# A two-layer fp32 transformer kernel: first query block over halves of the inputs, spatial sums in banks of two groups, and the last rows' norm weights from a row made in layer A

## The chip, the core and the metric

The kernel runs on one core of one Trainium2 chip. The metric is the device time of one execution in microseconds (us). TensorE is called PE, VectorE DVE, ScalarE ACT, GpSimd POOL and SyncE SP.

## The reference

The input is x, 512 rows (tokens) of 1024 numbers, and a memory of 256 rows. Two layers follow each other; everything is fp32.

```python
def rmsnorm(x, g):
    xf = x.astype(jnp.float32)
    y = xf * lax.rsqrt(jnp.mean(xf * xf, axis=-1, keepdims=True) + RMS_EPS)
    return (y * g.astype(jnp.float32)).astype(x.dtype)

def chunked_spatial_gating(u, v, w_s, b_s, ln_g, ln_b):
    u = jax.nn.gelu(u)
    v = layernorm(jax.nn.gelu(v), ln_g, ln_b)
    vc = v.reshape(B, nc, CHUNK, A_GROUPS, A_GROUP_DIM)          # 4 chunks of 128, 6 groups of 128
    w = jnp.where(mask[None], w_s, jnp.zeros((), w_s.dtype))     # lower triangle
    s = jnp.einsum('gts,bcsgd->bctgd', w, vc) + b_s.T[None, None, :, :, None]
    return u * s.reshape(B, S, MAIN_WIDTH)

for layer in range(2):
    a = rmsnorm(h, ln_mix_pre[layer])
    mem_n = rmsnorm(mem, ln_mem[layer])
    if layer == 0:                       # "layer A"
        proj = a @ w_in_a[layer]         # 1024 -> u 768, v 768, q_mem 256
        main = chunked_spatial_gating(u, v, ...)
    else:                                # "layer B"
        main = forgetting_attention(q, k_s, v_s, log_f_s)
    mixed = jnp.concatenate([main, memory_attention(q_mem, mem_n, w_mem_kv[layer])], axis=-1)
    h = h + rmsnorm(mixed @ w_out[layer], ln_mix_post[layer])
    f = rmsnorm(h, ln_ffn_pre[layer])
    f = (silu(f @ w_ffn_gate[layer]) * (f @ w_ffn_up[layer])) @ w_ffn_down[layer]
    h = h + rmsnorm(f, ln_ffn_post[layer])
```

The last line of layer B is the kernel's end: each row of f is divided by its root mean square, multiplied column by column by 1024 weights ("norm weights", gains), and added to h.

## The kernel before

**Numbers in two parts.** Each fp32 operand is split in a high part (a copy rounded to fp32r, by ACT) and a low part (the rest, by DVE): `whi` and `wlo` of weights, `ahi` and `alo` of the normed inputs, `vhi` and `vlo` of the spatial values. `mm3` makes a product from three matmuls: high x high, low x high, high x low (L193 to L195, in the order that the profile's rows show).

**Layout.** h is kept turned: 8 tiles (index k) of 128 columns of the model by 512 rows. PSUM holds tiles of 128 x 512 in banks of three groups, `mm` and `lg` with three banks each and `tr` with two; a new tile of a group takes the bank whose turn it is and waits until its old content has been read. `idle(n, ...)` issues n matmuls on zeros whose result nobody reads (L88).

**Order.** Each engine has a queue of its own that it works through in order. A scheduler places the instructions in these queues, mostly as the program is written; `high_priority` moves some ahead, and `behind(...)` or `issue_after` places an instruction after a named one on its queue. Loads go through SP's queue.

**Start.** `layer_a` loads the weights of two query blocks (`raws`, each 128 x 1024, 512 KB; block 0 in two halves of 256 KB) and x (8 tiles of 256 KB) and multiplies them: `outs[0]` and `outs[1]` each get 8 products by `mm3`, input by input, both outputs for each input. The sum of squares of x (`acc`), its mean over columns (`st`, a matmul on `avg`), the root (`r`, POOL) and its spread over partitions (`rb`) follow, while PE goes on with the value blocks (`v`).

**Spatial sums.** For each of six groups `spatial(g)` makes two sums `s` of two chunks each (L735, L736). Ahead of them come a transpose of the layernorm's weights (`vcols`, L757), and the `rows` products with which `bsp`, the bias, is completed on DVE (L768). `gate_inputs(m)` makes the u of the next group on PE (`ps`), and DVE and ACT finish it (`u`).

**End.** The last product (w_down of layer B) has four blocks `tb` of 128 rows, each in two halves `dh` of 512 columns. `tail(tb)` makes the products `y` (PE), adds partial sums (DVE, L816), squares (ACT, L819, with the sum of squares in `ss`), completes the mean square `v` (DVE, L821), takes the root `r` (POOL, L262) and scales y by r (ACT, L840). In the last block the second half is done in two pieces of 256 columns, and y is scaled in pieces by DVE (L835) and ACT (L836). `give(tb - 1, ...)`, called after the next block's `tail`, transposes y into h's layout (`yt`, PE, L847), multiplies by the norm weights, which then are one number per partition, and adds to h (DVE, L852, 128 x 128 at a time), and stores (L1369, 256 KB a store; the last block 128 KB a store on SP and ACT in turn).

Of the kernel before, what the change touches and what calls it, by code (L numbers as in the profile page):

```python
# [15 lines left out]
P = 128  # L16
T = 512
D = 1024
# [22 lines left out]
def hybrid(ctx: ExitStack, tc: tile.TileContext, i: dict, out: bass.AP):  # L41
# [6 lines left out]
    sp = ctx.enter_context(tc.tile_pool(name="small", bufs=8))  # L48
    pp = ctx.enter_context(tc.tile_pool(name="psum", bufs=3, space=PSUM))
# [515 lines left out]

    def layer_a():
# [18 lines left out]
        tokens(0, 1)  # L585
        query_weights(1, 0, 1024)
        tokens(1, 2)
        tokens(2, 4)
# [3 lines left out]
        last_a = tuple(last_parts)  # L592
        vg, evacs = {}, []
# [28 lines left out]
        with tc.tile_pool(name="sgu", bufs=1) as lp:  # L622
# [105 lines left out]
            def spatial(g):  # L728
                t = temp("s", (P, TB, P))
                for tp2 in range(2):  # L730
                    o = ps("lg", (P, 2, 2, P), s="s")
                    hi, lo = vp[g // 2, tp2]
                    c = slice((g % 2) * P, (g % 2 + 1) * P)
                    for n in range(2):
                        PE.matmul(o[:, n, :, :], hi[:, n, c], ws[g], start=True, stop=True)  # L735
# [22 lines left out]
            V.tensor_copy(vcols, o)  # L758

# [25 lines left out]
    def tail_of(xs, load, ys, eps=None, last=False):  # L785
# [12 lines left out]
        def tail(tb, halfway=None):  # L798
# [4 lines left out]
            c = slice(tb, tb + 1)  # L803
            final = last and tb == TB - 1
            two = small("two", 1) if final else None
            at = [(0, 0, 4), (1, 0, 2), (1, 2, 4)] if final else [(0, 0, 4), (1, 0, 4)]
            for n, (dh, m0, m1) in enumerate(at):
                if m0 == 0:
                    o = ps("lg" if dh else "mm", s="y")
                cols = slice(m0 * P, m1 * P)  # L810
                for k in range(nk):
                    w = [part[:, m0:m1, :] for part in ws[k // 2, dh][k % 2]]
                    end = token_products(o[:, cols], xs[k], w, tb, k == 0, k == nk - 1)
                y = ys[tb][dh][:, cols]
                with urgent(tb):
                    V.tensor_add(y, o[:, cols], y)  # L816
# [3 lines left out]
                    if n == len(at) - 1:  # L820
                        V.scalar_tensor_tensor(out=v[:, c], in0=one, scalar=run, in1=eps[:, c] if eps is not None else rms_eps,  # L821
# [10 lines left out]
            if final:  # L832
                for m in (0, 2):
                    cols = slice(m * P, (m + 2) * P)
                    V.tensor_scalar_mul(ys[tb][1][:, cols], ys[tb][1][:, cols], r[:, c])  # L835
                    A.activation(ys[tb][0][:, cols], ys[tb][0][:, cols], AF.Copy, scale=r[:, c])  # L836
                return end
            with urgent(tb):
                for y in ys[tb]:
                    A.activation(y, y, AF.Copy, scale=r[:, c])  # L840

        return tail, ys

    def turned(ys, k, tbs, out):

        for n, tb in enumerate(tbs):
            PE.transpose(out[:, n * P : (n + 1) * P], ys[tb][k // 4][:, k % 4 * P : (k % 4 + 1) * P], ident)  # L847
# [510 lines left out]

    def give(tb, order, queues=(nc.sync,)):
# [79 lines left out]
```

## Time and profile before

| what | value |
|---|---|
| median of 3 runs | 1113.27 us (1113.27 to 1113.5) |
| the profiled execution | 1111.68 us, of which the span of its instructions 1110.0 us |
| PE, DVE, ACT, POOL busy | 99%, 81%, 60%, 2% of the span |
| moved by DMA | 118.13 MB, mean 106 GB/s |
| granted clock of TensorE | 0.999 |

The profiled execution is one of its own, 1.6 us below the median of the three timed ones; all places in the span below are of it. A row of the timeline has the start in us from the span's beginning, the busy time in us, the engine, the program's line, the operation, the tiles written and read, the shape, how many follow each other, and in brackets how long the engine was idle before and what ended that. A row of windows has, for each engine, the busy us and the instructions begun, then the clock of TensorE, the share in which the DMA engines were busy, and GB/s.

### The profile page before, as it was taken

The page shows a single profiled execution, that of the slowest core. Times are in us where ns is not written, and L with a number is a line of the kernel's source. Part 1 is how long each engine was busy: PE and PEld are TensorE (multiplying, and loading weights), DVE is VectorE, ACT ScalarE, POOL GpSimd, SP SyncE. Part 2 cuts the span into 40 slices and gives each one's busy share as a digit, 9 for nine tenths or more (in the row PEclk, how much of TensorE's full clock was granted, in tenths as well). Part 3 has the DMA queues.
Part 4 walks back from the last instruction along what each step waited for, and adds up shares of the span by engine and source line. Part 5 has one row for each costly group of instructions (what it writes and reads, how often), then busy time and mean ns, then how long its engine had stood idle before and what let it go on. Part 6 is the DMA issues. An engine that isn't in the chain of part 4 may idle for free.

```text
span 1110.0 us, 19527 instructions
## 1 busy us (share of the span) xinstructions
PE 1100.9 (99%) x7384; PEld 999.7 (90%) x7385; DVE 895.0 (81%) x1734; ACT 667.1 (60%) x1401; POOL 25.1 (2%) x41
## 2 busy tenths in 40 slices
PE   9999999999999999999999999999999999999998
PEld 6997889999899899998988897889999899899996
DVE  7879659897698598787868889868897698588775
ACT  7776578664366254477647667768665266254453
POOL 0000000000000000001000000000000000000000
PEclk9999999999999999999999999999999999999999
DMA  7521331334135133245222555431234134233222
GB/s 268 159 79 58 113 116 39 115 115 136 55 115 152 56 96 115 79 150 173 77 76 75 155 124 131 129 115 39 77 97 151 58 115 134 58 114 114 77 76 77
DMA packets 63558, 118.13 MB, mean 106 GB/s; under 512 B 5164, under 2 KB 39992, under 8 KB 63464
## 3 DMA queue, kind: packets, MB, share of 16 engines
q1 hardware_dynamic: 62584, 116.05, 34.4%
q8 instruction: 58, 0.95, 0.4%
q0 software_dynamic: 192, 0.52, 0.2%
q10 hardware_dynamic: 688, 0.31, 0.1%
q14 instruction: 36, 0.29, 0.1%
HBM read 104.71 MB, written 2.10 MB: 96 GB/s over the span
## 4 chain that ended last, share of the span: by engine, by line
PE 86%; DVE 3%; ACT 1%; issue 1%; DMA 0%; POOLq 0%; POOL 0%; DVEq 0%; ACTq 0%
PE y L193 10%; PE y L194 10%; PE y L195 10%; PE a L194 5%; PE a L195 5%; PE a L193 5%; PE ps L193 3%; PE ps L194 3%; PE ps L195 3%; PE x L194 3%; PE x L195 3%; PE x L193 3%; PE e L193 3%; PE e L194 3%; PE e L195 3%; PE tr L457 1%
## 5 line engine op out<-in xcount | busy, mean ns | idle before, releaser
L241 ACT CAST whi<-raw 128x512 fp32r<-128x512 f32 x460 | 277.2, 620 | 266.6 <-PE y L195 118.5
L241 DVE TENSOR_TENSOR wlo<-raw,whi 128x512 fp32r<-128x512 f32 x460 | 306.3, 686 | 117.0 <-ACT whi L241 114.6
L193 PE MATMUL y<-whi,fhi 128*128 128x512 f32 (+1 forms) x356 | 139.7, 393 | 0.0
L194 PE MATMUL y<-wlo,fhi 128*128 128x512 f32 (+1 forms) x356 | 139.5, 392 | 0.0
L195 PE MATMUL y<-whi,flo 128*128 128x512 f32 (+1 forms) x356 | 139.1, 391 | 0.0
L194 PE MATMUL x<-xslo,whi 128*128 128x256 f32 x320 | 89.9, 281 | 0.0
L194 PE MATMUL a<-xslo,whi 128*128 128x256 f32 x320 | 89.9, 281 | 0.0
L195 PE MATMUL x<-xshi,wlo 128*128 128x256 f32 x320 | 89.8, 280 | 0.0
L193 PE MATMUL x<-xshi,whi 128*128 128x256 f32 x320 | 89.7, 280 | 0.0
L195 PE MATMUL a<-xshi,wlo 128*128 128x256 f32 x320 | 89.7, 281 | 0.0
L193 PE MATMUL a<-xshi,whi 128*128 128x256 f32 x320 | 89.6, 280 | 0.0
L195 PEld LDWEIGHTS y<-whi,flo 128*128 128x128 f32 x356 | 66.9, 188 | 15.5 <-DVE flo L241 0.2
L193 PEld LDWEIGHTS y<-whi,fhi 128*128 128x128 f32 x356 | 66.9, 188 | 15.1 <-DVE y L816 0.2
L194 PEld LDWEIGHTS y<-wlo,fhi 128*128 128x128 f32 x356 | 66.9, 188 | 14.7 <-DVE wlo L241 0.2
L193 PE MATMUL ps<-xshi,whi 128*128 128x256 f32 (+1 forms) x224 | 68.4, 306 | 0.0
L194 PE MATMUL ps<-xslo,whi 128*128 128x256 f32 (+1 forms) x224 | 66.7, 298 | 0.0
L195 PE MATMUL ps<-xshi,wlo 128*128 128x256 f32 (+1 forms) x224 | 66.4, 298 | 0.0
L193 PEld LDWEIGHTS a<-xshi,whi 128*128 128x128 f32 x320 | 60.3, 189 | 0.4
L194 PEld LDWEIGHTS a<-xslo,whi 128*128 128x128 f32 x320 | 60.2, 188 | 0.3
L193 PEld LDWEIGHTS x<-xshi,whi 128*128 128x128 f32 x320 | 60.3, 188 | 0.0
L195 PEld LDWEIGHTS x<-xshi,wlo 128*128 128x128 f32 x320 | 60.2, 188 | 0.0
L194 PEld LDWEIGHTS x<-xslo,whi 128*128 128x128 f32 x320 | 60.2, 188 | 0.0
(289 smaller groups left out, 3082.1 us busy)
## 6 DMA issues: line engine op xcount, KB each, us to landing
raw<-in_w_gate SPq DMA_DIRECT2D x44, 512.0 KB
raw<-in_w_up SPq DMA_DIRECT2D x44, 512.0 KB
raw<-in_w_down SPq DMA_DIRECT2D x44, 512.0 KB
raw<-in_w_out SPq DMA_DIRECT2D x16, 512.0 KB
raw<-in_w_b_q SPq DMA_DIRECT2D x8, 512.0 KB
raw<-in_w_a_v SPq DMA_DIRECT2D x6, 512.0 KB
raw<-in_w_a_u SPq DMA_DIRECT2D x6, 512.0 KB
raw<-in_w_v SPq DMA_DIRECT2D x6, 512.0 KB
```

Of the source, the lines that this page charges most:

```text
L193: PE.matmul(o, w[0], x[0], start=start, stop=False, skip_group_check=more)
L194: PE.matmul(o, w[0], x[1], start=False, stop=False, skip_group_check=more)
L195: return PE.matmul(o, w[1], x[0], start=False, stop=stop, skip_group_check=more)
L241: last_parts[:] = A.copy(hi, src), (eng or V).tensor_sub(lo, src, hi)
L457: PE.transpose(tr[:, at * P : (at + 1) * P], src, ident)
```

## The change

Three things change; the line numbers grow by 1 to 28 with it.

**1. Start.** The loads come in another order: the first half of block 0's weights, inputs 0 to 3 one by one, the first half of block 1's weights, the second half of block 0's, inputs 4 to 7 in two loads, the second half of block 1's. PE multiplies inputs 0 to 3 for both outputs, block 0 first, then 4 to 7. Two pairs of matmuls on zeros between products are gone.

**2. Spatial sums.** The second of the two sums stays in `lg`, the first goes to `mm`.

**3. End.** In layer A, `row_of_gains` turns the last norm's weights, which lie as 128 x 8, to 8 x 128 (a transpose on PE, a copy and a DMA by ACT) and writes them to DRAM. After the first row block of the last product `spread_gains` loads this row of 1024 numbers to all 128 partitions. For the last two row blocks DVE multiplies y by the row ahead of the transposes (`gained`), or, for the second half of the last block, by r and the row in one instruction; the addition to h then takes 2 or 4 tiles at once. The transposes of block 2 stand after the last product instead of between its pieces, its third addition after the last `v`, and six matmuls on zeros are left of eight.

```diff
         query_weights(0, 0, 512)
-        tokens(0, 1)
-        query_weights(1, 0, 1024)
-        tokens(1, 2)
-        tokens(2, 4)
+        for k in range(4):
+            tokens(k, k + 1)
+        query_weights(1, 0, 512)
         query_weights(0, 512, 1024)
         tokens(4, 6)
         tokens(6, 8)
         last_a = tuple(last_parts)
+        query_weights(1, 512, 1024)
...
             outs = [ps(t) for t in ("mm", "lg")]
-            for k in range(KT):
+            for half in range(0, KT, 4):
                 for o, w in zip(outs, wq):
-                    end = mm3(o, w[k], a[k], k == 0, k == KT - 1)
-                    if k == 0:
-                        idle(2, zero, end)
+                    for k in range(half, half + 4):
+                        mm3(o, w[k], a[k], k == 0, k == KT - 1)
...
-                    o = ps("lg", (P, 2, 2, P), s="s")
+                    o = ps(("mm", "lg")[tp2], (P, 2, 2, P), s="s")
...
+    def row_of_gains(block):
+        gain_row[0] = dp.tile([KT, P], F32, name="row")
+        o, row = ps("tr", (KT, P), s="gr"), temp("row", (KT, P))
+        PE.transpose(o, gains[:, block * KT : block * KT + KT], ident)
+        A.copy(row, o)
+        nc.scalar.dma_start(gain_row[0], row)
+
+    def spread_gains():
+        row = gain_row[0]
+        gain_row[0] = wp.tile([P, D], F32, tag="raw", name=name("raw"), bufs=4)
+        nc.sync.dma_start(gain_row[0], row.rearrange("a b -> (a b)").partition_broadcast(P))
...
             V.tensor_copy(vcols, o)
+            row_of_gains(G_FFN_POST + 1)
...
+            added = last and tb >= TB - 2
             final = last and tb == TB - 1
+            if added:
+                gained[tb] = [plain("yg") for _ in range(2)]
...
-                if m0 == 0:
-                    o = ps("lg" if dh else "mm", s="y")
-                cols = slice(m0 * P, m1 * P)
+                cols, own = slice(m0 * P, m1 * P), slice(0, (m1 - m0) * P)
+                o = ps("lg" if dh > m0 else "mm", s="y")
...
-                    V.tensor_add(y, o[:, cols], y)
+                    V.tensor_add(y, o[:, own], y)
+                    if added and not (final and dh):
+                        V.tensor_mul(gained[tb][dh][:, cols], y, gain_row[0][:, 512 * dh + m0 * P : 512 * dh + m1 * P])
...
             if final:
                 for m in (0, 2):
                     cols = slice(m * P, (m + 2) * P)
-                    V.tensor_scalar_mul(ys[tb][1][:, cols], ys[tb][1][:, cols], r[:, c])
-                    A.activation(ys[tb][0][:, cols], ys[tb][0][:, cols], AF.Copy, scale=r[:, c])
-                return end
+                    y0, y1 = (y[:, cols] for y in gained[tb])
+                    V.scalar_tensor_tensor(out=y1, in0=ys[tb][1][:, cols], scalar=r[:, c],
+                                           in1=gain_row[0][:, 512 + m * P : 512 + (m + 2) * P],
+                                           op0=ALU.mult, op1=ALU.mult)
+                    A.activation(y0, y0, AF.Copy, scale=r[:, c])
+                return end, total
             with urgent(tb):
-                for y in ys[tb]:
+                for y in gained[tb] if added else ys[tb]:
                     A.activation(y, y, AF.Copy, scale=r[:, c])
...
+    def give_added(tb, order, tags, queues=(nc.sync,), end=None, held={}):
+        c = (tb * P, (tb + 1) * P)
+        for n, some in enumerate(order):
+            tr = ps(tags[n], (P, len(some), P), s="yt")
+            k0, k1 = some[0], some[-1] + 1
+            with behind([end] if end else ()):
+                for x, k in enumerate(some):
+                    row_turned(gained[tb], k, tr[:, x, :])
+            with behind(held.get(n, ())):
+                V.tensor_add(h[:, k0:k1, c[0] : c[1]], tr, h[:, k0:k1, c[0] : c[1]])
+            queues[n % len(queues)].dma_start(out[:, k0:k1, c[0] : c[1]], h[:, k0:k1, c[0] : c[1]])
...
     for tb in range(TB):
-        end = tail(tb)
-        if tb:
+        end, sums = tail(tb)
+        if tb == 0:
+            spread_gains()
+        elif tb < TB - 1:
             give(tb - 1, (range(4), range(4, 8)))
-    idle(8, zero, end)
-    give(TB - 1, (range(4, 6), range(2), range(6, 8), range(2, 4)), (nc.sync, nc.scalar))
+    give_added(TB - 2, (range(2), range(2, 4), range(4, 8)), ("tr", "tr", "mm"), end=end, held={2: [sums]})
+    idle(6, zero, end)
+    give_added(TB - 1, (range(4, 6), range(2), range(6, 8), range(2, 4)), ("lg", "mm") * 2, (nc.sync, nc.scalar))
```

On PE, the first query block stood thus before (ps_181 and ps_182 are the two outputs, ahi_118 and alo_119 the parts of input 0, the next even and odd numbers those of input 1):

```order
L193 MATMUL ps_181<-ahi_118,whi_138 128x512
L194 MATMUL ps_181<-alo_119,whi_138 128x512
L195 MATMUL ps_181<-ahi_118,wlo_139 128x512
L88 LDWEIGHTS zeros_76
L88 MATMUL idle_186<-zeros_76 128x512
L88 LDWEIGHTS zeros_76
L88 MATMUL idle_186<-zeros_76 128x512
L193 MATMUL ps_182<-ahi_118,whi_146 128x512
L194 MATMUL ps_182<-alo_119,whi_146 128x512
L195 MATMUL ps_182<-ahi_118,wlo_147 128x512
```

Now (ps_185 and ps_186 are the outputs, ahi_120 is of input 0, ahi_126 of input 3), from the fourth input on:

```order
L194 MATMUL ps_185<-ahi_126,whi_140 128x512
L194 MATMUL ps_186<-ahi_120,whi_157 128x512
L195 MATMUL ps_185<-alo_127,whi_140 128x512
L196 MATMUL ps_185<-ahi_126,wlo_141 128x512
L195 MATMUL ps_186<-alo_121,whi_157 128x512
L196 MATMUL ps_186<-ahi_120,wlo_158 128x512
L194 MATMUL ps_186<-ahi_122,whi_157 128x512
```

The second output (its weights whi_157, wlo_158) now begins after ten products of the first instead of after three, and the matmuls on zeros between are gone; its third product is the 15th of the 48.

On DVE, the last block's end stood thus before (y_9720 is the second half of the last row block, yt_13440 the second half of block 2 turned, v the mean square):

```order
L816 TENSOR_TENSOR y_9720<-y_13392,y_9720 128x256
L852 SCALAR_TENSOR_TENSOR h<-yt_13440,gains,h 128x128 x2
L821 SCALAR_TENSOR_TENSOR v_13182<-ss_13181,two_13375,eps_13177 128x1
L852 SCALAR_TENSOR_TENSOR h<-yt_13440,gains,h 128x128
L835 TENSOR_SCALAR y_9720<-y_9720,r_13183 128x256 x2
L852 SCALAR_TENSOR_TENSOR h<-yt_13440,gains,h 128x128
L852 SCALAR_TENSOR_TENSOR h<-yt_13459,gains,h 128x128 x2
```

Now (y_9724 is that half, yt_13444, yt_13449 and yt_13454 are block 2, raw_13267 is the row of weights):

```order
L835 TENSOR_TENSOR y_9724<-y_13422,y_9724 128x256
L1397 TENSOR_TENSOR h<-yt_13444,h 128x2x128
L1397 TENSOR_TENSOR h<-yt_13449,h 128x2x128
L842 SCALAR_TENSOR_TENSOR v_13186<-ss_13185,two_13387,eps_13181 128x1
L1397 TENSOR_TENSOR h<-yt_13454,h 128x4x128
L857 SCALAR_TENSOR_TENSOR yg_13386<-y_9724,r_13187,raw_13267 128x256 x2
L1397 TENSOR_TENSOR h<-yt_13473,h 128x2x128
```

All of block 2's additions now stand behind the last y, two of them ahead of v and one behind it, each over two or four tiles.

More of the change, by code (lines that the diff above doesn't have):

```diff
@@ L48, in hybrid @@
     sp = ctx.enter_context(tc.tile_pool(name="small", bufs=8))
+    dp = ctx.enter_context(tc.tile_pool(name="rows", bufs=1, space=bass.MemoryType.DRAM))
     pp = ctx.enter_context(tc.tile_pool(name="psum", bufs=3, space=PSUM))
@@ L563, in mem_heads @@
         return heads
+    gained, gain_row = {}, [None]
+    def row_of_gains(block):
[8 more added lines that the diff above has]
+        nc.sync.dma_start(gain_row[0], row.rearrange("a b -> (a b)").partition_broadcast(P))
     def layer_a():
@@ L820, in tail @@
                     if n == len(at) - 1:
-                        V.scalar_tensor_tensor(out=v[:, c], in0=one, scalar=run, in1=eps[:, c] if eps is not None else rms_eps,
+                        total = V.scalar_tensor_tensor(out=v[:, c], in0=one, scalar=run, in1=eps[:, c] if eps is not None else rms_eps,
                                                op0=ALU.add, op1=ALU.add)
@@ L846, in turned, with row_turned @@
         for n, tb in enumerate(tbs):
-            PE.transpose(out[:, n * P : (n + 1) * P], ys[tb][k // 4][:, k % 4 * P : (k % 4 + 1) * P], ident)
+            row_turned(ys[tb], k, out[:, n * P : (n + 1) * P])
+    def row_turned(y, k, out):
+        PE.transpose(out, y[k // 4][:, k % 4 * P : (k % 4 + 1) * P], ident)
     def residual(o, k, cols, post):
```

3 lines of the change are left out of this document (2 added, 1 removed).

## The prediction

> **What bounds the kernel now.** I read the page's engine table first, then the view of waits of TensorE (PE), then the timeline around each edited place.
>
> ```profile
> span 1110.0 us, 19527 instructions
> PE 1100.9 (99%) x7384; PEld 999.7 (90%) x7385; DVE 895.0 (81%) x1734; ACT 667.1 (60%) x1401; POOL 25.1 (2%) x41
> ...
> PE s L735 <- DVE bsp L768: 1.1, 1, 1.1
> PE ps L193 <- ACT ahi L245: 0.3, 1, 0.3
> ```
>
> The rows of waits give total, count and longest in us. PE is busy 99% of the span, and one wait in mid-kernel is over 1 us. So what shortens PE's stream moves everything behind it, and only PE's own gaps, its matmuls without use, and the tail behind its last product can be gained.
>
> **The start.** The first query block is 48 products of 512 columns (8 inputs, 2 outputs, 3 products each).
>
> ```profile
> 1.25 3.97 PE L88 MATMUL idle<-zeros 128*128 128x512 bf16 x10 [1.25 <-DVE zeros L80]
> 5.56 0.50 PE L193 MATMUL ps<-ahi,whi 128*128 128x512 f32 x1 [0.34 <-ACT ahi L245]
> 8.46 0.61 PE L88 MATMUL idle<-zeros 128*128 128x512 bf16 x2
> 10.16 0.39 PE L193 MATMUL ps<-ahi,whi 128*128 128x512 f32 x1
> ...
> 19.02 0.40 PE L195 MATMUL ps<-ahi,wlo 128*128 128x512 f32 x1
> ...
> 3.86 0.62 ACT L241 CAST whi<-raw 128x512 fp32r<-128x512 f32 x1 [1.11 <-DMA raw<-in_w_a_q]
> 4.79 0.72 ACT L245 ACTIVATE ahi<-h,gains 128x512 fp32r<-128x512 f32 x1 [0.31 <-DMA h<-in_x]
> 6.72 1.14 ACT L241 CAST whi<-raw 128x512 fp32r<-128x512 f32 x2 [1.21 <-DMA raw<-in_w_a_q]
> 8.02 0.72 ACT L245 ACTIVATE ahi<-h,gains 128x512 fp32r<-128x512 f32 x1 [0.16 <-DMA h<-in_x]
> 9.29 1.34 ACT L245 ACTIVATE ahi<-h,gains 128x512 fp32r<-128x512 f32 x2 [0.55 <-DMA h<-in_x]
> ...
> 8.77 0.75 DVE L246 SCALAR_TENSOR_TENSOR alo<-h,gains,ahi 128x512 fp32r<-128x512 f32 x1
> ...
> 9.00:12.00 3.00, 2.72 (x12) 1.99 (x11) 2.75 (x7) 2.63 (x5) 0.00 (x0) 1.00 1.01 383
> ```
>
> The 10.16 product is the 10th, the 19.02 one the 48th: (19.02 - 10.16) / 38 = 0.233 us each, with no gap. Ahead of that PE waits for loads, and the last row (a window: busy times, clock 1.00, DMA share 1.01, 383 GB/s) says that the DMA engines are full. So ACT's five waits date the bytes: 256 KB of weights at 3.86, 512 KB in all at 4.79, 1024 at 6.72, 1280 at 8.02, 1792 at 9.29.
>
> In the new order the first weights serve four inputs. On the same curve inputs 1, 2, 3 land at 5.75 (half way from 512 to 1024 KB), 6.72 and 8.02, the second output's weights at 8.65 (half way to 1792) and the first output's second half at 9.29. ACT casts input 3 until 8.74 and those weights until 9.36. DVE ends input 3's low part at 9.52, does a small copy (0.16 us between starts) and then the weights' low part (0.69 a piece) to about 10.35. That is what PE's row 15 of the new order waits for; the 14 ahead have their operands by 9.5. From there 34 products remain, the last starting at 10.35 + 33 x 0.233 = 18.05, against 19.02. The later loads hold: inputs 4 and 5 (2304 KB) land at about 10.65 and their low parts are done by 12.1 and 12.8, PE wants them at 12.7 and 13.4; the last weights' low part is done by 14.9 and wanted at 15.5. The four matmuls without use lie in waits, so their removal alone is worth nothing. Gain 0.97.
>
> What follows is less covered, since ACT and DVE finish 0.15 to 0.4 later (they wait for the same bytes with more still to do), while PE comes 0.97 earlier:
>
> ```profile
> 17.92 5.68 DVE L279 TENSOR_TENSOR acc<-acc,sq 128x512 f32<-128x512 f32 x8
> 23.73 0.95 PE L290 MATMUL st<-avg,acc 128*128 128x1 f32 x8
> 24.97 1.41 POOL L262 TENSOR_TENSOR r<-var,mhalf 128x4 f32<-128x4 f32 x1 [22.04 <-DVE var L293]
> 27.22 0.60 PE L259 MATMUL rb<-ident,r 128*128 128x128 f32 x4
> 40.17 0.62 ACT L241 CAST whi<-raw 128x512 fp32r<-128x512 f32 x1 [1.05 <-PE ps L194]
> ```
>
> Six of the eight additions are those of x, so the sum is done at 17.92 + 6 x 0.71 = 22.2; it becomes 22.4 to 22.6, and PE now asks at 22.76. The next, r, is done at 26.38 and asked for at 27.22, both of which move with st. At 40.17 ACT waits for PE again. I take off 0.1: start -0.85, bounds -0.4 (the second weights half a microsecond later) to -1.2 (the weights at 8.4, so that input 3 decides).
>
> **The spatial sums.**
>
> ```profile
> 95.03 0.23 PE L757 MATMUL vcols<-ident,vrows 12*128 12x12 f32 x1
> 95.19 1.55 PE L764 MATMUL rows<-ws,tri 128*128 128x128 f32 x12
> ...
> 98.33 0.36 PE L735 MATMUL s<-ws,vhi 128*128 128x256 f32 x1 [1.13 <-DVE bsp L768]
> ...
> 95.13 0.68 DVE L241 TENSOR_TENSOR vlo<-vg,vhi 128x512 fp32r<-128x512 f32 x1
> ...
> 97.33 0.85 DVE L768 SCALAR_TENSOR_TENSOR bsp<-rows,vcols,bsp 128x128 f32<-128x128 f32 x3
> 98.60 0.62 ACT L241 CAST vhi<-vg 128x512 fp32r<-128x512 f32 x1 [1.20 <-DVE vg L722]
> ...
> 95.00:100.00 5.00, 3.87 (x27) 3.51 (x27) 5.00 (x15) 3.15 (x6) 0.00 (x0) 1.00 0.01 2
> ```
>
> Two "rows" tiles and the first sum hold the three lg banks, so the second sum waits until DVE has read the first rows (98.18). In the other group its bank is free, and its operand vlo was done at 95.81, so the 1.13 us go. What is late next: DVE is busy all of 95 to 100, and the following u, s and bsp pass through it. The waits that I followed to the first gate block have at least 0.9 us between DVE's end and PE's use; with PE 1.0 nearer this is just used up, so I leave 0.1 for it at the low end. The row made here costs PE one transpose (0.16 by the distance from vcols to rows), ACT a small copy and a DMA issue within its 1.20 us wait. PE: 1.13 - 0.13 = 1.0; bounds -0.6 to -1.1.
>
> **The end.**
>
> ```profile
> 1098.95 0.71 PE L847 MATMUL yt<-ident,y 128*128 128x128 f32 x5
> 1099.63 0.39 PE L193 MATMUL y<-whi,fhi 128*128 128x256 f32 x1
> 1101.05 0.28 PE L195 MATMUL y<-whi,flo 128*128 128x256 f32 x1
> ...
> 1094.06 0.69 DVE L816 TENSOR_TENSOR y<-y,y 128x512 f32<-128x512 f32 x1 [1.90 <-PE y L195]
> 1101.37 0.42 DVE L816 TENSOR_TENSOR y<-y,y 128x256 f32<-128x256 f32 x1 [0.54 <-PE y L195]
> 1102.37 0.22 DVE L821 SCALAR_TENSOR_TENSOR v<-ss,two,eps 128x1 f32<-128x1 f32 x1
> 1103.24 0.61 DVE L835 TENSOR_SCALAR y<-y,r 128x256 f32<-128x256 f32 x2 [0.40 <-POOL r L262]
> 1103.77 2.75 DVE L852 SCALAR_TENSOR_TENSOR h<-yt,gains,h 128x128 f32<-128x128 f32 x9
> ...
> 1104.00:1108.50 4.50, 1.41 (x8) 0.60 (x6) 2.45 (x9) 0.15 (x1) 0.00 (x0) 0.85 0.61 175
> ```
>
> Five transposes stand between the last two pieces; moved behind, they let the last product come 0.68 earlier (1099.63 - 1098.95), and DVE's last y at about 1100.7. Then, in the new order of DVE, stand two additions to h of 2x128 before v (0.42 each, as y of 256 columns). v needs ACT's square as well, which in the trace puts it 1.00 after y; the two additions end about 1.2 after y, so v starts at 1101.9, 0.47 earlier (in the old frame, without the gains ahead of it), and r and what follows with it. Behind r, DVE does one addition of 512 columns (0.69, inside POOL's time for r), two scalings (0.87 by the low parts' 0.47 at 256 columns) and four additions at 0.35, against the 3.28 us from 1103.24 to 1106.52 now: it ends at 1102.77 + 0.87 + 4 x 0.35 = 1105.1 instead of 1106.52. The three multiplications by the row lie in DVE's gaps (1.90 before 1094.06).
>
> The stores do not follow all the way. The last row moves 175 GB/s x 4.5 us = 788 KB, that is block 2's second half and block 3, and they run to 1108.0. Block 2 can now go from 1102.4 on; block 3's 524 KB from about 1104.9 at the window's full rate, 175 / 0.61 = 287 GB/s, need 1.83, and its last piece is issued only at 1105.2: end 1106.8 to 1107. I take -1.1; bounds -0.4 (stores bunch up as now) to -1.4 (DVE's whole gain).
>
> **Sum:** -0.85 - 1.0 - 1.1 = -2.95 on the profiled execution's 1111.68 us (span 1110.0). The median of the runs is 1113.27, 1.6 longer; I take the same difference there: 1110.3. From no change a measurement here tells some 0.2%, 2.2 us.
>
> **The rivals.** (1) Start not gained: st or the low parts hold PE, because DVE and ACT are no faster with the new order. For it speak the margin of 0.2 at st and the full DMA queues; against it, that five products more are done when PE becomes gapless. -2.1: 1111.2. (2) The end is given back: DVE's held additions put v where it was, or the stores bunch. For it speaks the 0.6 share with full slices; against it, that block 2 leaves two microseconds earlier. -1.9: 1111.4. (3) The clock. The first ten matmuls, of 512 columns too, take 0.40 each, the products from 10.16 on 0.233; PE is slow when it starts. Without four of its fillers PE is busy 14 x 0.233 = 3.3 of the 4.8 us from 5.56 to 10.35. If that makes it slow again at half the rate for as long as those ten, 3.97 us, 2.0 are lost, the start comes to +1.15 and the time to 1112.3. Against it: by the landings above no gap is over 0.8 us, and before the change PE went through gaps of 0.3 without slowing. The Trainium skill (TensorE: Matmul & The Clock Gate, Part 1) has the gate fall after an idle window of about 3.4 us; by that rule it stays up here, though its window runs freely. (4) Slower: the row's load. It is 512 KB from one 4 KB row to all partitions, queued on SP behind the last down weights, and it needs a weights buffer that has been cast.
>
> ```profile
> 1082.44 1.28 DVE L241 TENSOR_TENSOR wlo<-raw,whi 128x512 fp32r<-128x512 f32 x2
> ...
> 1074.00:1086.00 12.00, 12.00 (x63) 9.96 (x63) 7.71 (x14) 5.06 (x11) 0.00 (x0) 1.00 0.00 1
> ```
>
> The last casts end at 1083.7 and no DMA runs from 1074 to 1086 (share 0.00). At the 383 GB/s of the start, 524 KB take 1.4 us, so it would be there by 1086, eight us before the first use: DVE multiplies at the start of its 1.90 us idle time ahead of 1094.06. That multiplication stands ahead of all later work of DVE, whose slack up to 1094 is spent first; each microsecond later delays the tail by one, and from 1097 on the whole gain is gone. So it decides only if the row is read at under a ninth of that rate (524 KB in 13.3 us); at a tenth, say, it lands at 1097.7 and the time is 1114.0 with the other gains kept: 1113.27 - 2.95 + 3.7. (5) The sums still wait, on another bank's reader (u or gate products that still are in mm): -0.85 - 1.1 = -1.95, 1111.3. For it speaks DVE's full 95 to 100, against it that vlo and that bank were done by 95.81.
>
> **How the numbers follow.** All three terms within their bounds 0.60; (1) 0.12, (2) 0.12, (3) 0.05, (5) 0.06, (4) 0.05. Upper ends together, 3.7, give 1109.6, and 0.4 for the scatter between executions 1109.2; the top reaches to (3), 1112.3. What is left out is (4) and the chance that two terms beat their bounds. Faster by over 0.2% is the first case and part of the mixed ones, whose sums lie at the bound: 0.64; same 0.30; slower 0.06.
>
> **What would show it.** The last product of the first block near 18.05 with no idle rows; no wait on bsp in PE's waits, and PE's s rows close together; the last y product 1.85 + 0.68 earlier, at about 1098.5, DVE's last addition done at 1106.5 - 1.85 - 1.4 = 1103.3, and the span's end at 1107.05. The forecast is wrong if st shows a wait on acc, if the clock in 6 to 12 is under 1.00, or if DVE shows a wait for the row's DMA.

## The result, and the profile after

The changed kernel takes 1109.26 us (median of 6; 1108.6 to 1110.17) beside 1113.13 of the kernel before. The ratio is 0.9967 with a 95% interval of 0.9954 to 0.9979, that is -3.7 us (-5.1 to -2.3). Forecast were -2.95 us, 1110.3, and a range of 1109.2 to 1112.3. The profiled execution took 1109.59 us, with a span of 1107.9: 2.1 below that of before. So the one execution that each trace shows moved less than the median, and this difference is the main thing to explain. One execution of the kernel before, in group 3 of the experiments, took 1802 us at a mean granted clock of 0.556; it stands in no comparison here.

The page and PE's waits of the changed kernel:

```profile
span 1107.9 us, 19514 instructions
PE 1098.8 (99%) x7380; PEld 999.3 (90%) x7380; DVE 896.1 (81%) x1728; ACT 667.0 (60%) x1402; POOL 24.9 (2%) x41
...
PE tr L458 <- DVE p L451: 1.0, 1, 1.0
PE ps L194 <- ACT ahi L246: 0.9, 1, 0.9
PE ps L195 <- DVE alo L247: 0.6, 2, 0.3
...
PE yt L875 <- ACT yg L860: 0.2, 1, 0.2
```

The wait for bsp (1.1) is gone, and those of the end have shrunk from 0.8 in all to 0.2. Two have grown: 0.9 (before 0.3) for the high part of an input, here input 2, in the start, and 1.0 (before 0.2) far away in layer B, where a transpose waits for p.

The start, from the timeline of PE and ACT:

```profile
6.82 0.39 PE L194 MATMUL ps<-ahi,whi 128*128 128x512 f32 x1
8.75 0.50 PE L194 MATMUL ps<-ahi,whi 128*128 128x512 f32 x1 [0.92 <-ACT ahi L246]
18.96 0.39 PE L196 MATMUL ps<-ahi,wlo 128*128 128x512 f32 x1
...
7.98 1.34 ACT L246 ACTIVATE ahi<-h,gains 128x512 fp32r<-128x512 f32 x2 [1.72 <-DMA h<-in_x]
```

The last product of the first block starts at 18.96, not at 18.05: only 0.06 earlier than in the trace of before. Input 2 was there at 7.98, not at 6.72. The chain of waits says that it is one transfer:

```profile
2.19 5.76 DMA h<-in_x
7.96 0.02 issue
7.98 0.73 ACT ahi L246
```

In the trace's records of landings, each load has 16 ends, as many as the core has DMA engines on the page. Of input 2, 15 ends had come by 6.56, the last at 7.96; of input 3 by 7.21 and 8.58; of the second weights by 8.20 and 9.26. From input 2 on the last end came 1.1 to 1.4 us behind the 15th. That it is one and the same engine each time is a reading: the records do not name it.

The sums, and the end:

```profile
95.36 0.27 PE L573 MATMUL gr<-ident,gains 128*8 128x128 f32 x1
...
97.16 0.22 PE L752 MATMUL s<-ws,vlo 128*128 128x128 f32 x1
97.22 0.33 PE L751 MATMUL s<-ws,vhi 128*128 128x256 f32 x1
...
97.68 0.45 PE L194 MATMUL ps<-ahi,whi 128*128 128x512 f32 x1
...
1099.28 0.28 PE L196 MATMUL y<-whi,flo 128*128 128x256 f32 x1
1099.40 1.04 PE L875 MATMUL yt<-ident,yg 128*128 128x128 f32 x8
...
1099.60 0.42 DVE L835 TENSOR_TENSOR y<-y,y 128x256 f32<-128x256 f32 x1 [0.22 <-PE y L196]
1099.94 0.75 DVE L1397 TENSOR_TENSOR h<-yt,h 128x256 f32<-128x256 f32 x2
1100.65 0.22 DVE L842 SCALAR_TENSOR_TENSOR v<-ss,two,eps 128x1 f32<-128x1 f32 x1
1101.53 0.88 DVE L857 SCALAR_TENSOR_TENSOR yg<-y,r,raw 128x256 f32<-128x256 f32 x2
1102.56 1.42 DVE L1397 TENSOR_TENSOR h<-yt,h 128x256 f32<-128x256 f32 x4 [0.15 <-PE yt L875]
...
1103.50:1104.00 0.50, 0.00 (x0) 0.00 (x0) 0.48 (x2) 0.00 (x0) 0.00 (x0) 1.00 0.05 13
1104.00:1104.50 0.50, 0.00 (x0) 0.00 (x0) 0.00 (x0) 0.00 (x0) 0.00 (x0) 1.00 1.00 285
1105.50:1106.00 0.50, 0.00 (x0) 0.00 (x0) 0.00 (x0) 0.00 (x0) 0.00 (x0) 1.00 0.62 181
```

The second sum follows the first without a gap. From vcols to the next u product PE took 95.20 to 97.68, 2.48 us, where it took 95.03 to 98.82, 3.79, before: 1.31 less, with the new transpose inside. The new transpose itself cost 0.03: from vcols to the first rows product PE takes 0.19, before 0.16. At the end DVE's last addition is done at 1103.98 (before 1106.52) and the stores at about 1105.8 (before 1108.0).

To see where PE gains and loses between these places, I laid the matmuls of two traces side by side, in their order, and took the difference of their start times, each counted from the beginning of its own span. The changed kernel stands against before at -0.07 behind the first block, +0.18 at 93 us, -1.15 behind the sums, -1.45 from 250 us on, -0.7 at 690, 0.0 behind the wait for p, -1.0 at 1097 and -1.8 behind the last product.

### The profile page after: what moved, and what is told of

Same layout as the page of the kernel before. It is cut to its first block, busy times and chain, and to the rows that moved or that the text cites. A ratio compares the mean times of both kernels' runs of the same rounds, so it can differ in the third digit from the quotient of the medians.

```text
span 1107.9 us, 19514 instructions
## 1 busy us (share of the span) xinstructions
PE 1098.8 (99%) x7380; PEld 999.3 (90%) x7380; DVE 896.1 (81%) x1728; ACT 667.0 (60%) x1402; POOL 24.9 (2%) x41
## 4 chain that ended last, share of the span: by engine, by line
PE 94%; DVE 2%; ACT 1%; DMA 1%; issue 1%; SPq 1%; POOLq 0%; POOL 0%; DVEq 0%; ACTq 0%
PE y L194 10%; PE y L195 10%; PE y L196 10%; PE a L194 5%; PE a L196 5%; PE a L195 5%; PE ps L194 4%; PE ps L195 4%; PE ps L196 4%; PE e L196 3%; PE e L194 3%; PE e L195 3%; PE x L196 3%; PE x L194 3%; PE x L195 3%; PE v L194 2%
## 5 line engine op out<-in xcount | busy, mean ns | idle before, releaser
L196 PEld LDWEIGHTS a<-xshi,wlo 128*128 128x128 f32 x320 | 60.2, 188 | 0.0
```

The source lines that it names most:

```text
L196: return PE.matmul(o, w[1], x[0], start=False, stop=stop, skip_group_check=more)
```

## The experiments

Twelve kernels were run, in three groups of four; a group shares its runs of the kernel before, and each ran on another chip, so that across groups only ratios are compared closely. The ratios are those on record, with their 95% intervals; they are not the quotients of the two medians. "Long" below is an execution 1.3 us or more above the shortest one of its kernel and group.

| kernel | runs | median (us) | shortest | long | ratio to before |
|---|---|---|---|---|---|
| before, group 1 | 29 | 1112.09 | 1111.00 | 10 | |
| E1 start alone | 11 | 1112.13 | 1110.16 | 7 | 0.9994 (0.9986 to 1.0003) |
| E2 banks alone | 11 | 1110.41 | 1110.08 | 0 | 0.9984 (0.9976 to 0.9993) |
| E3 end alone | 11 | 1110.61 | 1109.96 | 3 | 0.9984 (0.9976 to 0.9993) |
| E4 the changed kernel again | 6 | 1108.62 | 1108.22 | 2 | 0.9966 (0.9955 to 0.9978) |
| before, group 2 | 24 | 1112.15 | 1111.25 | 10 | |
| E5 before, wait filled | 11 | 1111.90 | 1111.57 | 2 | 0.9996 (0.9987 to 1.0005) |
| E6 changed, five fillers | 8 | 1110.13 | 1109.56 | 0 | 0.9976 (0.9966 to 0.9986) |
| E7 changed, old start | 5 | 1108.92 | 1108.82 | 0 | 0.9965 (0.9953 to 0.9978) |
| E8 before, no fillers | 11 | 1112.96 | 1111.01 | 7 | 0.9997 (0.9988 to 1.0006) |
| before, group 3 | 34 | 1111.94 | 1111.22 | 13 | |
| E9 before, longer wait | 11 | 1112.30 | 1111.74 | 2 | 1.0001 (0.9993 to 1.0010) |
| E10 changed, three fillers | 11 | 1109.88 | 1109.19 | 1 | 0.9979 (0.9971 to 0.9988) |
| E11 before, one more load | 11 | 1111.78 | 1110.86 | 4 | 0.9995 (0.9987 to 1.0004) |
| E12 before, transposes moved | 12 | 1114.47 | 1112.87 | 7 | 1.0021 (1.0013 to 1.0030) |

**E1, the start alone.** The kernel before with only the first two pieces of the diff (the order of the loads, the loop over halves without `idle`).

> The kernel before with the new start alone. Theory A (the prediction's term): -0.85 us, so about 1112.3 where before stands at 1113.15, and the first query block's last product about 0.9 before that of before. Theory B (from one trace of the changed kernel, where one of the 16 DMA engines ended each load 1 to 1.4 us after the other 15): the new order wins only in executions without such a late engine, on average -0.3 or less. In the trace the last product of the block then stands at 18.0 where the loads of inputs 2 and 3 land by 7.3, and at 18.9 where they land at 8 or later.

The median did not move; the ratio is 0.9994, -0.7 us with an interval of -1.6 to +0.3, which holds both no change and the forecast. The shortest executions are 0.8 shorter than before's, but seven of eleven are long. The profiled one (1112.83) is a long one, and it shows why. In it the start did gain: the last product of the block stands at 18.39, with inputs 2 and 3 landed by 7.38 and 8.04. Then comes the wait for bsp as before, and behind it this, in windows of 1 us:

```profile
PE s L734 <- DVE bsp L767: 1.1, 1, 1.1
...
98.00:99.00 1.00, 1.00 (x6) 0.90 (x7) 1.00 (x5) 0.83 (x2) 0.00 (x0) 0.61 0.00 0
99.00:100.00 1.00, 1.00 (x4) 0.81 (x3) 1.00 (x3) 0.62 (x2) 0.00 (x0) 0.50 0.02 8
100.00:101.00 1.00, 1.00 (x4) 0.81 (x3) 1.00 (x4) 0.75 (x2) 0.00 (x0) 0.50 0.00 0
101.00:102.00 1.00, 1.00 (x4) 0.76 (x4) 1.00 (x3) 0.48 (x1) 0.00 (x0) 0.68 0.00 0
...
99.42 0.63 PE L195 MATMUL ps<-ahi,wlo 128*128 128x512 f32 x1
99.84 0.63 PE L193 MATMUL ps<-ahi,whi 128*128 128x512 f32 x1
```

The third number from the right is the granted clock. It falls to 0.50 right behind the wait and stays there to about 101.6, some 3.4 us; products stand 0.42 apart instead of 0.233, and by the side-by-side difference 1.5 us are lost (-0.43 at 93 us, +1.05 at 113). This is theory D: a wait may cost its own length and, in part of the executions, a further 1.5 us. It was formed on this run; the expectations from E5 on carry it.

The mean granted clock of every execution speaks for it too. One fall of 3.4 us to a half is 0.0015 of the span. Of before's 87 executions, all 33 long ones have a mean clock of 0.997 or 0.998; of the other 54, 46 have 0.999 or 1.000, seven 0.998 and one 0.948. So before's long executions lost clock; where in the program, these means do not say. Not every long execution is such a fall: of E1's seven, three have 0.999.

**E2, the banks alone.** One line: `ps("lg", ...)` to `ps(("mm", "lg")[tp2], ...)`.

> The kernel before with only the spatial sums' banks changed. Theory A: -1.13 (the whole wait, without the row's transpose), about 1112.0, and no wait for bsp in PE's waits. Theory B (the wait comes back within the next microseconds, since DVE is full from 95 to 111): PE's u products or later sums show waits on DVE of 0.5 or more in all, and the time moves by 0.5 or less.

The time moved by -1.8 (-2.7 to -0.8). No wait came back: against before's trace the difference goes from +0.36 at 93 us to -0.97 at 113 and -1.35 at 1097; the step between, at 250 us, is in nearly all traces against before's. None of eleven executions is long, where 33 of 87 of before are. So the wait itself is worth 1.1 to 1.3. The rest of the 1.8 would be the clock's fall behind it, which goes too; the interval alone does not separate the two, but beside before's 19 executions that are not long (median 1111.58) E2's median is 1.2 less.

```profile
97.34 0.22 PE L736 MATMUL s<-ws,vlo 128*128 128x128 f32 x1
97.40 0.33 PE L735 MATMUL s<-ws,vhi 128*128 128x256 f32 x1
```

**E3, the end alone.** The diff's end, with `row_of_gains` in layer A.

> The kernel before with the new end alone, with the row made in layer A (its transpose lies in the wait for bsp and costs nothing here). Theory A (prediction): -1.1, about 1112.05. Theory B (the stores hold it up): -0.4 to -0.6. Theory C (the end is worth more than the prediction says, since block 2's stores no longer stand ahead of block 3's): -1.8 or more; the median of the changed kernel, 3.9 below that of before, asks for 1.8 here if the start brings 0.9 and the sums 1.1.

-1.8 (-2.7 to -0.8) by the ratio; in the trace the span is 1108.9 against 1110.0, though PE comes to the end 0.22 later than in before's trace (at 1097 us). So this execution gains 1.3 at the end, a little more than the prediction's 1.1; the shortest executions differ by 1.04. Theory C's 1.8 lies within the interval, but no row shows it. DVE's last additions, like those of the changed kernel:

```profile
1102.74 0.88 DVE L858 SCALAR_TENSOR_TENSOR yg<-y,r,raw 128x256 f32<-128x256 f32 x2
1103.78 1.42 DVE L1398 TENSOR_TENSOR h<-yt,h 128x256 f32<-128x256 f32 x4 [0.15 <-PE yt L876]
```

**E4, the changed kernel again.**

> The changed kernel once more, with a trace of its own. If the parts add, its time is before plus the three differences of the other runs here. Theory A: -2.95, 1110.2. The first timing gave -3.87 with an interval of about -2.3 to -5.1. In the trace: theory B of the start expects a last product of the first block between 18.0 and 19.0, by the landing of the slowest DMA engine; a wait of 1.0 us of a transpose of p on DVE at 705 us, seen in the first trace of the changed kernel and not in that of before, is scatter if it is gone here.

0.9966, the first timing again. The parts' ratios give -0.7 - 1.8 - 1.8 = -4.3, the whole -3.8 (-5.0 to -2.5): they add within their uncertainty. The profiled execution (1110.61) is the longest of the six, and now the clock falls in the start:

```profile
8.02 0.50 PE L194 MATMUL ps<-ahi,whi 128*128 128x512 f32 x1 [0.69 <-ACT ahi L246]
8.80 0.62 PE L195 MATMUL ps<-alo,whi 128*128 128x512 f32 x1 [0.28 <-DVE alo L247]
20.46 0.39 PE L196 MATMUL ps<-ahi,wlo 128*128 128x512 f32 x1
...
8.00:9.00 1.00, 0.70 (x2) 0.39 (x3) 0.96 (x2) 0.97 (x2) 0.00 (x0) 1.00 1.06 397
9.00:10.00 1.00, 1.00 (x3) 0.78 (x3) 1.00 (x2) 0.98 (x2) 0.00 (x0) 0.52 1.03 406
11.00:12.00 1.00, 1.00 (x4) 0.81 (x3) 0.69 (x2) 0.69 (x2) 0.00 (x0) 0.50 1.03 358
12.00:13.00 1.00, 1.00 (x4) 0.80 (x4) 0.93 (x2) 0.87 (x3) 0.00 (x0) 0.78 1.02 412
```

Two gaps of 0.69 and 0.28 us between products, then half clock from 9.04 to 12.45. The eight distances of products from 9.21 to 12.55 take 3.34 us, 1.5 more than at 0.233 each. The block ends at 20.46, outside the 18.0 to 19.0 of theory B, and 1.4 later than before: the prediction's third rival, in one of two traces of this kernel. Gaps alone do not decide it: the other trace has a longer one, 0.92, and no fall. The wait for p at 694 us is there again, 0.5, so it was no accident of one execution.

**E5, the wait filled.** In `spatial(0)`, after the first sum:

```diff
+                    if g == 0 and tp2 == 0:
+                        with tc.issue_after(end.ins):
+                            f = ps("tr", s="fill")
+                            for _ in range(4):
+                                PE.matmul(f, tri[:, 384:], tri, start=True, stop=True)
```

> The kernel before with four matmuls of 512 columns on constants, whose result nobody reads, put into PE's wait between the two first spatial sums (4 x 0.233 = 0.93 of the 1.13 us). The wait itself stays. Theory A (the wait costs its own 1.13 us and no more): no change, the same scatter of 3 us as before. Theory D (in some executions the clock of TensorE halves after this wait for about 3.4 us and costs 1.6 us more; seen at 98.4 to 101.7 in the trace of the start alone): the shortest executions as before, 1111.0 to 1111.5, but none of the nine in 29 above 1112.9; the median 0.3 to 0.7 lower.

Two of eleven are long, against 10 of 24 of before; the median is 0.25 lower, the interval includes no change. It points the way theory D says, but neither is it none, as expected, nor is 2 in 11 told apart from 10 in 24 by so few.

**E6 and E10, fillers back in the changed start.** In E6 `idle(2 + k, zero, end)`, in E10 `idle(1 + k, zero, end)`, behind the first two products (k = 0 and 1):

```diff
                     for k in range(half, half + 4):
-                        mm3(o, w[k], a[k], k == 0, k == KT - 1)
+                        end = mm3(o, w[k], a[k], k == 0, k == KT - 1)
+                        if o is outs[0] and k < 2:
+                            idle(1 + k, zero, end)
```

> The changed kernel with matmuls on zeros back in the start: two behind the first product, three behind the second, of 0.22 us each, in PE's waits for inputs 1 and 2. Theory A (the fillers are worth nothing, as the prediction says): no change or up to 0.3 longer. Theory D (without them the clock halves in some executions from about 9.0 to 12.5 us, as in the second trace of the changed kernel): the short executions as now, 1108.2 to 1108.7, and none of those at 1109.5 to 1110.6; median about 1108.5, 0.3 to 0.8 below the changed kernel's.

> The changed kernel with three matmuls on zeros in the start: one behind the first product, two behind the second (five were too many: in their trace they held up the third product by 0.4 to 0.6). Theory D: no execution at 1109.5 or more, the shortest at 1108.2 to 1108.5 as without fillers, median 1108.5, ratio 0.996. Theory E (the new start costs what it gains later in the program, and the fillers cost again): 1109.5 or more, not below the changed kernel.

Long executions nearly vanish, one of nineteen beside 3 of 12 of the changed kernel (too few to tell apart), but the shortest are 1.0 to 1.3 longer than the changed kernel's 1108.22, and the ratio is worse by 1.1 to 1.4 us (0.9976 and 0.9979 against 0.9966; the intervals overlap). Theory E's time, not its reason: in E10's trace the start is the best of all, with no wait and the last product at 18.24,

```profile
8.49 0.58 PE L194 MATMUL ps<-ahi,whi 128*128 128x512 f32 x1
18.24 0.39 PE L196 MATMUL ps<-ahi,wlo 128*128 128x512 f32 x1
```

0.78 ahead of before's, though its shortest execution is no match for the changed kernel's. What it loses later is in no wait: from 253 to 1097 us its difference to before rises from -2.02 to -1.37, while E2's, E3's and E8's stand still to 0.08. E6's rises in the same way. The distances of single matmuls differ there from before's, mostly by up to 5 ns either way, and the sum is a loss; in the changed kernel, E1 and E4 the pattern is another one, the same in all three, and without such a loss at the end. Why, the records do not show; it stays open.

**E7, the old start in the changed kernel.** Sums and end as changed, the first part of the diff undone.

> The changed kernel with the start of before (its order of loads and products and its four fillers); sums and end as changed. Theory A: the start is worth 0.85, so 1109.5 or more. Theory D: its executions lie close together (no wait after which the clock falls), at 1109.0 to 1109.8, so its median is about 0.7 above the shortest of the changed kernel and within 0.5 of the changed kernel's median.

0.9965 against the changed kernel's 0.9966 and 0.9967: no worth of the start is seen. Each of these ratios is known to 1.3 us or so only, so 0.85 is not excluded by them. The five executions lie within 0.8 us. The changed kernel's shortest in E4's group is 0.6 shorter, its longest 1.0 longer. That is theory D's picture.

**E8, before without its fillers.** Only `if k == 0: idle(2, zero, end)` is taken out of the first block's loop.

> The kernel before without the four matmuls on zeros between the first products, nothing else. Theory A (they lie in waits and are worth nothing): no change within 0.3. Theory D: in part of the executions the clock halves in the start too, so more executions at 1113 to 1114 and some at 1115, and the median 0.3 to 1 above before.

The shortest are not longer without the fillers (1111.01 beside 1111.25), so the fillers cost nothing that shows; the median is 0.8 higher and seven of eleven are long, as in E1. The ratio's interval still includes no change. In the trace of a long one (1113.0) the clock falls not in the start but behind the wait for bsp again, from 98.6 to 102.0:

```profile
98.00:99.00 1.00, 0.60 (x3) 0.64 (x4) 1.00 (x4) 0.34 (x1) 0.00 (x0) 0.79 0.00 0
100.00:101.00 1.00, 1.00 (x4) 0.72 (x3) 1.00 (x5) 0.40 (x2) 0.00 (x0) 0.50 0.00 0
```

So why fillers 85 us earlier should matter is not shown; 7 of 11 may be chance.

**E9, a longer wait.** Two copies from PSUM ahead of DVE's reading of the first rows:

```diff
+                for _ in range(2 * (1 - n)):
+                    V.tensor_copy(temp("slow", (P, 384)), o)
```

> The kernel before with two extra copies (128 x 384 out of PSUM, some 0.9 us together) on DVE ahead of its reading of the first rows, so that PE's wait for bsp grows from 1.13 to about 2.0 us. Theory A (a wait costs its own length): +0.9, about 1113.0, with the same share of executions 1.6 above the shortest as before. Theory D (the longer PE stands, the surer TensorE's clock halves for 3.4 us behind it): nearly all executions are in the long group, +0.9 + 1.6, about 1114.5, and the trace shows a granted clock of 0.5 between about 99 and 102.5.

The scheduler put two of the next u products ahead of the waiting sum, so the wait grew to 1.5 only:

```profile
PE s L735 <- DVE bsp L770: 1.5, 1, 1.5
```

The time is +0.1 (-0.8 to +1.1) and two of eleven are long. Theory D in its simple form, the longer the wait the surer the fall, is refuted: at 1.55 us nearly all executions should be long, and 2 of 11 are. The two products in between kept PE busier, so what counts may be how busy PE is over a stretch of some microseconds.

The kept traces bear this out. The changes of the clock lie on a grid: in every trace they come a whole number of 3.413 us after the clock's first rise (in E1 the rise is at 6.07 us and the fall at 98.23, 27 steps later), and the first rise lies anywhere from 4.1 to 6.5 us. In E1 and E8 a line of the grid lies 0.35 and 0.17 us behind the end of the wait, so one stretch holds the whole wait and the small products ahead of it. In the traces that have the wait and no fall there, the nearest line lies 0.4 to 1.6 us ahead of its end (before, E3, E9, E12) or 1.0 behind it (E11). As an estimate of how full a stretch is I take the columns of its matmuls at 0.233 us for 512: 0.37 of the stretch ahead of the fall in E1, 0.34 in E8, 0.34 in E4. Of all other stretches of the fourteen traces up to 1095 us the emptiest, the changed kernel's first with its gap of 0.92, has 0.41, and none is followed by a fall; E9's, with its two products, has 0.45. Behind 1095 us, where transposes are much of the work, the estimate does not separate them: the changed kernel has a stretch of 0.35 there (from 1101.0) without a fall. By this reading, where the grid happens to lie decides whether a wait costs more than its length. It was made from the traces afterwards, and no run tested it.

**E11, one more load.** `tokens(2, 4)` as `tokens(2, 3)` and `tokens(3, 4)`.

> The kernel before with inputs 2 and 3 loaded one by one instead of together, nothing else: one more DMA on SP's queue at the start, as the changed start has. It asks where the changed start loses 0.3 to 0.7 us at 694 us (PE tr waiting for DVE p, 0.5 to 1.0 in all traces with the new start, 0.2 in those without). Theory F (one more DMA shifts the place of a stall of SP's issue that every trace has, to the issue of qc<-whi at 681 to 684, 1.3 to 1.5 us there against 0.5): the same wait of 0.5 to 1.0 appears here, and PE's spacing drifts by some 0.7 us between 250 and 550 as in those traces. Theory G (PE's or ACT's instructions do it): wait 0.2, no drift. Time: F +0.4, G within 0.2.

No change, no drift, and the wait is 0.2: theory F falls as far as the number of loads goes.

```profile
PE tr L457 <- DVE p L450: 0.2, 1, 0.2
```

What the wait for p hangs on is visible in the trace of the changed kernel: SP took 1.47 us to issue one small transfer (0.46 in before's), the next were late, and ACT waited for one of them ahead of p. The row of before comes first, then two of the changed kernel:

```profile
682.39 0.46 SPq L1311 DMA_DIRECT2D qc<-whi  x1
...
681.68 1.47 SPq L1339 DMA_DIRECT2D qc<-whi  x1
689.98 0.62 ACT L242 CAST whi<-raw 128x512 fp32r<-128x512 f32 x1 [0.63 <-DMA qa<-whi]
```

The long issue was there in the changed kernel's two traces, E1's and E6's (new start), weaker in E5's (old start) and not in E10's (new start). What puts SP's stall there stays open.

**E12, the transposes moved alone.** `give(TB - 2, ...)` after the last `tail`, its transposes behind the last product, `idle(6)`; the weights stay one number per partition.

> The kernel before with block 2's eight transposes behind the last product and six matmuls on zeros after them, but with the norm weights per partition as before (no row, 16 additions of 128 x 128 with scaling). Theory A (prediction's terms): the last product 0.68 earlier, v about 0.4 earlier, but DVE has 8 additions of 0.28 after the last y instead of 5, so its end at most 0.1 to 0.4 earlier and the time -0.1 to -0.4; of the end's 1.1 the row's wider additions bring the larger part. Theory H (the place of the transposes alone brings it): -0.8 or more.

+2.3 us (+1.5 to +3.3), the side on which neither theory was. PE's waits in it:

```profile
PE idle L88 <- DVE h L852: 2.0, 1, 2.0
...
PE y L193 <- DVE y L816: 0.5, 1, 0.5
...
1106.00:1107.00 1.00, 1.00 (x5) 0.55 (x3) 0.35 (x2) 0.00 (x0) 0.00 (x0) 0.50 0.90 247
```

The second is the reason why the last product did not come earlier at all: without the transposes between, the last piece of y waits until DVE has read the piece ahead of it, since both lie in one bank. The first and what follows: block 2's transposes hold both tr banks until DVE's 128 x 128 additions have read them, and the matmuls on zeros and the last block's transposes queue behind the same two banks. Behind the 2.0 us wait the granted clock is 0.50 from 1105.3 on, so the last transposes run at half clock; part of the 2.3 us is that. So moving the transposes pays only with the other bank for the last piece and the wide additions in other groups of banks.

## Why the prediction was right, point by point

**What bounds the kernel:** right. What PE gained at the sums stayed to the end in E2 and E7. With the new start, matmul distances added or took several tenths of a microsecond without any wait, which the prediction did not have.

**The start, -0.85:** the term that held least. Alone it measured -0.7 (-1.6 to +0.3), and E7 shows nothing of it, so its worth is not settled. In the traces the last product of the block stands at 19.02 to 19.67 in the nine with the old start or a variant of it (E8, E11), of which before's is the earliest, and at 18.24 to 18.96 in four of the five with the new one; E4, with the fall, has 20.46. Three steps failed. "On the same curve inputs 1, 2, 3 land at ...": the curve came from one execution's waits. Input 2, forecast at 6.72, landed at 7.07 to 8.01 in the five traces with the new start, in the changed kernel's first because of one late end out of 16. Where inputs 2 and 3 came early enough (E1, E10) the last product stood at 18.39 and 18.24, near the forecast 18.05. Second, "the four matmuls without use lie in waits, so their removal alone is worth nothing" left out what they do for the clock: the stretch ahead of E4's fall was 0.34 full without them. That putting them back helps is not shown (E6, E10). Third, in the rival on the clock, "no gap is over 0.8 us" was taken as safe; gaps of 0.69 and 0.28 were enough in E4. That rival's loss was put at 2.0, its chance at 0.05. E4's trace lost about 1.5, and 3 of 12 executions of the changed kernel were long. The rule of the Trainium skill quoted there (TensorE: Matmul & The Clock Gate, Part 1: the gate falls after an idle window of about 3.4 us) does not agree with E4 if idle means without any work, since the longest idle time there was 0.69; the length of the slow stretch, 3.41 us, does agree with its window. The margin at st was no problem: PE's waits have no row for it.

**The sums, -1.0:** the mechanism right, the size too small for the median. The sums took 1.31 less, and the transpose cost 0.03 where 0.13 was taken off for it; no later wait on DVE took the gain back. What failed is "so the 1.13 us go" as the whole price: 33 of 87 executions of before are 1.3 us or more above the shortest, all with a mean clock of 0.998 or less, and in the two traces with this wait and a fall (E1, E8) the halved clock stands right behind it. That it does so in before's own long executions is inferred: before's one trace is not a long one. E2 measured -1.8 (-2.7 to -0.8).

**The end, -1.1:** right in the traces: six with the new end show 1.1 to 1.3 (span, less PE's difference at 1097). With PE 1.0 ahead when it began, DVE's end was forecast at 1106.5 - 1.0 - 1.4 = 1104.1 and stands at 1103.98; the stores' end at 1108.0 - 1.0 - 1.1 = 1105.9, where the window from 1105.5 is 62% full. The 1.83 us for the last 524 KB at full rate came true: 285 GB/s from 1104.0. Its step "moved behind, they let the last product come 0.68 earlier" is right only together with the second bank, which the prediction passed over (E12).

**The row's load, the slower rival:** it was issued at 1069.59 and landed by 1073, 18 us ahead of its first use at 1091.2.

**The sum:** 1110.3 was in error by +1.0 against the median and by -0.9 against the profiled execution (1109.59 instead of 1108.73). Start and wait for p cost the profiled execution more than forecast; the vanished falls of the clock, as far as the runs show, gave the median more. These are two errors of about one microsecond on opposite sides, and that the range held the result is partly luck.

No version beat the changed kernel. E7 equals it with less scatter (in five runs) and less change, so of the three parts the sums and the end carry the gain, and the start's share is not told apart from none.

## What to carry to other kernels

Price a wait of a busy TensorE from several executions, not from one: look for executions that are longer by the same step, and for a granted clock of 0.5 behind the wait; removing the wait may be worth more than its length. Before taking out matmuls without use, ask what they do for the clock in the executions where the loads come late. A load that a start depends on is there with the last of its 16 ends, so read that one, in several executions, and leave a microsecond.

## What the runs showed of the hardware

TensorE's clock fell to half for 3.41 us after waits of only 1.1 us (E1, E8) and after gaps of 0.69 and 0.28 us (E4), in some executions and not in others of the same program; each fall cost about 1.5 us. A longer wait of 1.55 us, with two products ahead of it, did not make it more frequent (2 of 11). The changes lie on a grid of 3.413 us whose place differs from execution to execution; the three falls followed stretches that by the estimate of E9 were 0.34 to 0.37 full, and none followed a stretch that was 0.41 full or more (up to 1095 us, fourteen traces).

The last of a load's 16 ends can come 1.1 to 1.4 us behind the 15th (inputs 2 and 3 and the second weights in the changed kernel's first trace); single packets of 2 KB, 84 ns at the median, took up to 1.05 us there.

Programs with the new start have matmuls whose distance differs, mostly by up to 5 ns, from before's over hundreds of microseconds. The pattern is the same in both traces of the changed kernel (their difference moves by 0.07 us from 33 to 690 us) and in E6 and E10 (0.09), and it adds up to 0.6 to 1.0 us up or down. The cause is open.
